# One layer of a hybrid streaming encoder: x enters transposed and unscaled, w_out writes channels on partitions, and the choice of standard and seven-product jobs changes

## Chip, cores and metric

The kernel runs on one core of one Trainium2 chip. The metric is device time in microseconds (us) for one execution; the median of several runs counts. Five things work side by side: TensorE (PE, with its weight loads PEld), VectorE (DVE), ScalarE (ACT), GpSimd (POOL, idle here) and SyncE (SP), which issues all DMAs.

## The reference

A layer for 1024 tokens of 1024 channels, everything in float32:

```
h = rms_norm(x, norm1_w);  proj = h @ w_in            # 1024 -> 7168
q, k, v, g_ret, x_lru, y_lru, gate_ret, gate_lru = split(proj)
y_a = (group_norm(retention(rotary(q), rotary(k), v)) * silu(g_ret)) @ w_ret_o
y_b = (rg_lru(conv(x_lru)) * gelu(y_lru)) @ w_lru_o
mix = sigmoid(gate_ret + b0) * y_a + sigmoid(gate_lru + b1) * y_b
x = x + mix @ w_out
gate, val = split(rms_norm(x, norm2_w) @ ffn_w_up)    # 1024 -> 2 x 3072
x = x + (gelu(conv(gate)) * val) @ ffn_w_down         # 3072 -> 1024
return rms_norm(x, norm_f_w)
```

## The kernel before

**Precision.** Every large product runs in three passes of a 32-bit matmul: each operand is split into a rounded part and the rest (`split`: a ScalarE copy `hi`, L569, and a VectorE subtraction `lo`, L570), and `hi·hi + hi·lo + lo·hi` is accumulated (`PASSES`). A matmul takes a 128x128 stationary block and 512 moving columns.

**Jobs.** The projections are cut into jobs of 256 output channels (28 in w_in, 4 each in ret_o and lru_o, 24 in up; 12 in down, by 3 groups g of 1024 input channels and 4 sets t of token tiles). The weight of a job comes in four blocks A11, A12, A21, A22 (output half, input half), the other operand in B11 to B22 (input half, token half). A *standard* job (`mm_std`, matmuls on L632) makes the four outputs one after the other, 24 matmuls of each. A *fast* job (`mm_fast`, L650) is Winograd's form of Strassen's product: seven block products of 12 matmuls. It takes block sums S1 to S4 of the weight, which VectorE makes in the job (L590 to L599), and T1 to T4 of the operand, which are made once for all jobs that share it; B12 itself occurs in no product. Sums of products are put together in banks X, Y and Z, with copies out by ScalarE (`keep`, L658) and additions on VectorE (`total`, L668). Of one job the products come in the order A11·B11, S1·T1, S2·T2, A12·B21, S3·T3, A22·T4, S4·B22, and `run` puts the first product of the next fast job with the same operand ahead of A22·T4 (`ahead`).

**Stages.** Ahead of the first job `xload` and `norm_half` load x by tokens, take sums of squares, scale the tokens, transpose on TensorE (L749) into channels on partitions and split; `tsets` makes T1 to T4. Then the jobs of w_in in the order of `SEQ`: q, k, v and gate of a head (h), the two branches of the recurrence (x, y), and the merge gates (g); the first STD_L = 2 are standard. Retention and recurrence are side work: generators that `advance` steps on between products, written out to DRAM as og and u. ret_o: 4 standard jobs. lru_o: one standard job, three fast ones. w_out: 384 matmuls (L1174) with mix as the stationary operand, tokens on partitions, first the left 512 output channels, then the right ones; x is added, x1 goes to DRAM, and for each token half `norm_half` normalises and transposes again (L749, tile a). Up: STD_U = 1 standard job, 23 fast. The block sums of w_down are made in the up stage (`down_sums`) and go through DRAM (td). Down: in each of three groups one standard and three fast jobs, adding to x1 in DRAM; the last group ends in the final norm.

**Order.** `record` writes the program down as operations on named tiles. `Prog.plan` goes through them from the end and gives each a latest start; `Prog.run` plays the engines forward with its own durations and takes, for each engine that is free, the ready operation with the earliest latest start. Main TensorE work keeps its order, side work may go between. A tile needs one of 100 buffers of 128x512 (kind u), 6 PSUM banks (g) or 2 for side work (a). What comes out is the fixed instruction order of every engine; on the chip only semaphores decide.

Of the kernel before, what the change touches and what calls it, by code (L numbers as in the profile page):

```python
# [88 lines left out]
class VT:  # L89


    __slots__ = ("kind", "shape", "dt", "acc", "real", "slot", "left", "plan", "name", "whole", "tracked")
# [21 lines left out]
class Ref:  # L114

    __slots__ = ("base", "ops", "shape", "box")

    def __init__(self, base, ops=(), shape=None, box=None):
        self.base, self.ops = base, ops
        self.shape = tuple(base.shape) if shape is None else shape  # L120
        self.box = box

    def __getitem__(self, idx):
        t = idx if isinstance(idx, tuple) else (idx,)
        t = t + (slice(None),) * (len(self.shape) - len(t))
        shape, box = [], []
        for n, i in zip(self.shape, t):
            if isinstance(i, slice):
                a, b, _ = i.indices(n)
                shape.append(b - a)  # L130
                box.append((a, b))
            else:
                box.append((i, i + 1))
        return Ref(self.base, self.ops + (("get", idx),), tuple(shape),
                   tuple(box) if self.box is None and not self.ops else self.box)
# [44 lines left out]
class Op:  # L180

    __slots__ = ("eng", "how", "args", "kw", "occ", "lat", "pred", "succ", "allocs", "uses", "pos", "ls",
                 "start", "ready", "side", "i", "tab", "slack", "dma", "line")
# [17 lines left out]
class Prog:  # L201
# [3 lines left out]
    def __init__(self):  # L205
        self.ops = []
        self.t = 0.0
        self.side = False
        self.slack = None
        self.after = []  # L210

    def add(self, eng, how, args, kw, line):
# [3 lines left out]
        o.side, o.slack = self.side, self.slack  # L216
# [124 lines left out]
    def run(self, caps, trace=None):  # L341
        ops = self.ops
        self.plan()
        STEP = 500.0
# [14 lines left out]
        for v, (s, e) in vts.items():  # L359
            v.plan = s  # L360
            if v.kind == "u":
                occ[bin_(s):bin_(e) + 1] += 1
# [20 lines left out]

        def can(o, t):
            need = [v for v in o.uses if v.slot is None]
            for v in need:
# [3 lines left out]
                if v.kind == "u":  # L390
                    now = t - slip
                    if now < v.plan:
                        if now < v.plan - self.EARLY or len(f) <= self.SPARE:
                            return False
# [5 lines left out]
        def start(o, t):  # L400
# [7 lines left out]
            if o.dma:  # L408
                arrive = max(t + 700, dma_free)
                dma_free = arrive + o.dma / 262144 * 950  # L410
                lat = max(dma_free + 900 - t, 2300.0)
# [5 lines left out]
            for v in o.allocs:  # L417
                _, v.slot = heapq.heappop(free[v.kind])
                if v.kind == "u":
                    now = t - slip  # L420
                    if now < v.plan:
                        occ[bin_(now):bin_(v.plan)] += 1
            for v in o.uses:
                v.left -= 1
                hold[v] = max(hold.get(v, 0.0), done)
                if v.left == 0:
                    heapq.heappush(free[v.kind], (hold[v] + 60, v.slot))
                    heapq.heappush(events, hold[v] + 60)
            for q, l in o.succ:
# [59 lines left out]
        return order  # L489
# [3 lines left out]
    SPARE = 5  # L493
    SWITCH = 1500.0
    LOOK = 12

    def emit(self, engines, make):
        at = {}
        for o in self.order:
# [14 lines left out]
         ("x1", (T, D)), ("td", (3, 4, 4, P, TH)), ("ff", (3, 8, 2, P, 4, P)))  # L514
# [5 lines left out]
STD_L = 2  # L520
STD_U = 1
RATE = 1.0
SEQ = "g g y0 g y1 h0 h1 h2 h3 x0 g g x1 g y2 g x2 g y3 x3"


class Job:

    def __init__(self, src, op, emit, post=None, fast=True, pre=None, fetch=None):
        self.src, self.op, self.emit, self.post = src, op, emit, post
        self.fast, self.pre, self.fetch = fast, pre, fetch  # L530
        self.got = {}

    def take(self, m, h):
        return self.got.pop((m, h)) if (m, h) in self.got else self.fetch(m, h)


def record(prog, fx):
# [4 lines left out]
    og_d, u_d, y_d, sg_d, t1_d, x1_d, td_d, ff_d = (  # L542
        fx[n] for n in ("og_d", "u_d", "y_d", "sg_d", "t1_d", "x1_d", "td_d", "ff_d"))
    x, positions, normf, w_in, w_ro, w_lo, w_out, w_up, w_dn, w_gate, out = (
        fx[n] for n in ("x", "positions", "normf", "w_in", "w_ro", "w_lo", "w_out", "w_up", "w_dn", "w_gate", "out"))
# [61 lines left out]
    def advance(budget):  # L607
        budget *= max(1, len(back))
        while back and budget > 0:
            with within(4000.0, True):  # L610
                c = next(back[0], None)
            if c is None:
# [8 lines left out]
    def mm_std(jb, op):  # L621
        block = blocks(jb)
        for m in range(2):
            for h in range(2):
                ps = bank()
                n = 0
                for k in range(KT):
                    w = block(f"A{m + 1}{k // 4 + 1}")
                    c = slice(128 * (k % 4), 128 * (k % 4) + 128)
                    o = op[f"B{k // 4 + 1}{h + 1}", k % 4]  # L630
                    for a, b in PASSES:
                        PE.matmul(ps, w[a][:, c], o[b], start=n == 0, stop=n == 23)  # L632
                        n += 1
                    if k % 4 == 3:
                        advance(RATE)
                with within(3000.0):
                    jb.emit(m, h, ps, None)

    def mm_fast(jb, op):
# [3 lines left out]
        def prod(ps, an, bn, first):  # L643
            w = block(an)
            n = 0
            for j in range(4):
# [14 lines left out]
        def more(u, m, c):  # L661
            if jb.pre is not None and (m, c) in jb.pre:
                with within(3000.0):
                    V.tensor_add(u, u, jb.take(m, c))
# [17 lines left out]
        u3 = keep(X)  # L682
        more(u3, 1, 1)
        total(u3, Z, 1, 1)
        yield
# [3 lines left out]
        more(u2, 0, 1)  # L689
        prod(Z, "S4", "B22", False)  # L690
        total(u2, Z, 0, 1)

    def run(jobs):
        ahead = None
        for jb, nx in zip(jobs, jobs[1:] + [None]):
            if jb.fast:
                g = ahead
                if g is None:
                    g = mm_fast(jb, jb.op)
                    next(g)  # L700
                next(g)
                ahead = None
                if nx is not None and nx.fast and nx.op is jb.op:
                    ahead = mm_fast(nx, nx.op)
                    next(ahead)
                next(g, None)
            else:
                mm_std(jb, jb.op)
            if jb.post is not None:
                g = jb.post()  # L710
                if g is not None:
                    back.append(g)
# [12 lines left out]
    def rms_scale(tiles, n, o=0):  # L725
        for t in range(n):
            for c in range(2):
                j = bank("a")
                if c == 0:
                    S.activation(j, tiles[t, c], AF.Square, accum_out=nst[:, c, o + t:o + t + 1])  # L730
                else:
                    V.scalar_tensor_tensor(j, tiles[t, c], 1.0, tiles[t, c], ALU.mult, ALU.mult,
                                           accum_out=nst[:, c, o + t:o + t + 1])
        a, b, v, r, w = (nst[:, i, o:o + n] for i in range(5))
        V.tensor_add(v, a, b)
        V.tensor_scalar(v, v, 1.0 / D, EPS, ALU.mult, ALU.add)
        rstd_of(r, v, w)
        return r

    def norm_half(tiles, wname, op, half, keep, wide=False):  # L740
        r = rms_scale(tiles, 4)
        for c in range(2):
            for t in range(4):
                V.tensor_scalar(tiles[t, c], tiles[t, c], r[:, t:t + 1], None, ALU.mult)
        for k in range(KT):
            ps = bank("g" if wide else "a")
            for t in range(4):
                c0 = 128 * (k % 4)
                PE.transpose(ps[:, 128 * t:128 * t + 128], tiles[t, k // 4][:, c0:c0 + 128], ident)  # L749
            w = pc(wname, k)  # L750
            hi, lo, f = get("hh", F32R), get("hl", F32R), get("hf")
            if k % 2 == 0:
                S.activation(hi, ps, AF.Copy, scale=w)
                V.scalar_tensor_tensor(lo, ps, w, hi.bitcast(F32), ALU.mult, ALU.subtract)
                S.activation(f, ps, AF.Copy, scale=w)
            else:
                S.activation(f, ps, AF.Copy, scale=w)
                V.tensor_copy(hi, f)
                V.tensor_sub(lo, f, hi.bitcast(F32))
            op[f"B{k // 4 + 1}{half + 1}", k % 4] = (hi, lo)  # L760
            keep[f"B{k // 4 + 1}{half + 1}", k % 4] = f
# [14 lines left out]
    def xload(half):  # L776
        tl = {}
        for t in range(4):
            for c in range(2):
                b = get("xt")  # L780
                r0 = 512 * half + 128 * t
                SY.dma_start(b, x[r0:r0 + 128, 512 * c:512 * c + 512])
                tl[t, c] = b
        return tl

    h1, keep = {}, {}
# [107 lines left out]
    def lru_block(n, xl):  # L894
# [7 lines left out]
        for h in range(2):  # L902
# [45 lines left out]
            for m in range(2):  # L948
# [15 lines left out]
                yield 1.7  # L964

# [76 lines left out]
    def ret_out(hd, gg):  # L1042
        for h in range(2):
            for m in range(2):
# [7 lines left out]
                yield 0.8  # L1052

    def emit_gate(which, n):
        def emit(m, h, src, unit):
            t = get("sg") if unit is None else unit
            S.activation(t, src, AF.Sigmoid, bias=pc("merge_gate_b", 8 * which + 2 * n + m))
# [3 lines left out]
    def operand(op, fetch, sums=True):  # L1061
# [3 lines left out]
        if sums:  # L1065
            tsets(op, fetch)
# [26 lines left out]
    def emit_ret_o(n):  # L1093
        def emit(m, h, ps, unit):
            t = ojobs[n].take(m, h)
# [4 lines left out]
    def emit_lru_o(n):  # L1100
        def emit(m, h, ps, unit):
            g, t = ojobs[4 + n].take(m, h)
# [7 lines left out]
    def add(i, emit, post=None):  # L1110
        jobs.append(Job(pair_src(w_in, i), h1, emit, post, fast=len(jobs) >= STD_L))

    gates = [(w, n) for n in range(4) for w in range(2)]
    for what in SEQ.split():
        if what == "g":
            w, n = gates.pop(0)
            add(20 + 4 * w + n, emit_gate(w, n))
# [13 lines left out]
    def start_tables():  # L1131
        lru_constants()
        return rotary_tables()
# [3 lines left out]
    ojobs = [Job(pair_src(w_ro, n), og, emit_ret_o(n), fast=False, fetch=from_sg(0, n)) for n in range(4)]  # L1137
# [264 lines left out]
```

## Time and profile before

| | us |
|---|---|
| median of 3 runs (1661.72 to 1663.68) | 1662.11 |
| the profiled execution | 1663.31 |
| its span, first to last instruction | 1661.5 |
| TensorE busy in the span | 1623.5 |
| VectorE busy | 1244.3 |
| ScalarE busy | 881.1 |
| first matmul of a job | 31.59 |
| end of the last matmul | 1653.4 |

How to read the views: a group is "line engine operation out<-in shapes xcount | busy us, mean ns of one | idle time before them and what ended it". In the chain and the timeline the first number is the start in us from the span's start, the second the length. In a table of windows each engine has its busy time with a count. Matmuls overlap, so the time that one adds to a full stream is the distance of two starts, not its duration.

### The profile page before, as it was taken

Reading aid. Unit: us, or ns where it says so; the run is one execution under the profiler, and the core shown is the slowest. Engines: PE = TensorE matmul, PEld = TensorE weight load, DVE = VectorE, ACT = ScalarE, POOL = GpSimd, SP = SyncE. Lnnn points to the kernel's source line nnn. Section 1 sums busy time; section 2 is a strip of 40 time slices with the busy share of each in tenths; the row PEclk is TensorE's granted clock in tenths of the full one; section 3 lists DMA queues with packets and bytes.
Section 4 is the critical chain, followed back from the end, with each engine's and each line's share of the span. In section 5 each row is a group of like instructions: output and inputs, shape, how many; then the busy total and the mean of one; then the engine's idle time right before and its main releaser. Section 6 shows DMA issues by size and latency. Waiting matters only on the chain.

```text
span 1661.5 us, 21070 instructions
## 1 busy us (share of the span) xinstructions
PE 1623.5 (98%) x7284; PEld 1339.1 (81%) x7284; DVE 1244.3 (75%) x2295; ACT 881.1 (53%) x1468; POOL 0.2 (0%) x4
## 2 busy tenths in 40 slices
PE   4999999999999999999999999999999999999997
PEld 4888888888888888888888788888888888888886
DVE  7986475766768887876882897777777777877786
ACT  6473434344578878863440464444444546544464
POOL 0000000000000000000000000000000000000000
PEclk9999999999999999999999999999999999999999
DMA  5343131322233336369454424344444448686862
GB/s 194 102 127 95 45 93 48 89 78 63 81 129 112 115 106 247 116 219 328 145 181 154 145 74 142 123 143 129 150 146 134 146 129 264 244 280 237 292 220 77
DMA packets 153804, 246.95 MB, mean 149 GB/s; under 512 B 15328, under 2 KB 40032, under 8 KB 153696
## 3 DMA queue, kind: packets, MB, share of 16 engines
q1 hardware_dynamic: 153696, 245.60, 45.2%
q8 instruction: 57, 0.93, 0.2%
q14 instruction: 51, 0.42, 0.1%
HBM read 173.19 MB, written 67.11 MB: 145 GB/s over the span
## 4 chain that ended last, share of the span: by engine, by line
PE 92%; ACT 4%; DVE 2%; DMA 1%; issue 1%; SPq 0%; DVEq 0%; ACTq 0%
PE g L650 68%; PE g L632 13%; PE g L1174 5%; PE a L928 2%; PE a L1018 1%; PE a L1025 1%; PE a L1017 1%; PE a L749 0%; PE a L1011 0%; PE a L1048 0%; PE a L1000 0%; DMA xt<-x 0%; ACT L947 0%; PE g L749 0%; DVE wl L570 0%
## 5 line engine op out<-in xcount | busy, mean ns | idle before, releaser
L650 PE MATMUL g<-bh,wh 128*128 128x512 f32 x1120 | 441.7, 394 | 3.5 <-ACT pk L658 3.4
L650 PE MATMUL g<-bh,wl 128*128 128x512 f32 x1120 | 440.2, 393 | 1.0 <-DVE wl L570 0.9
L650 PE MATMUL g<-bl,wh 128*128 128x512 f32 x1120 | 439.8, 393 | 0.2 <-DVE bl L570 0.2
L650 PEld LDWEIGHTS g<-bh,wh 128*128 128x128 f32 x1120 | 210.3, 188 | 48.4 <-ACT pk L658 5.9
L650 PEld LDWEIGHTS g<-bh,wl 128*128 128x128 f32 x1120 | 210.3, 188 | 45.5 <-DVE wl L570 3.0
L650 PEld LDWEIGHTS g<-bl,wh 128*128 128x128 f32 x1120 | 210.4, 188 | 42.7 <-DVE bl L570 0.7
L650 PE MATMUL g<-hh,wh 128*128 128x512 f32 x588 | 231.0, 393 | 0.0
L650 PE MATMUL g<-hh,wl 128*128 128x512 f32 x588 | 230.8, 393 | 0.0
L650 PE MATMUL g<-hl,wh 128*128 128x512 f32 x588 | 230.6, 392 | 0.0
L658 ACT COPY pk<-g 128x512 f32<-128x512 f32 x183 | 107.4, 587 | 218.5 <-PE g L650 212.8
L668 DVE TENSOR_TENSOR pk<-g,pk 128x512 f32<-128x512 f32 x183 | 126.2, 690 | 127.8 <-PE g L650 113.0
L569 ACT CAST wh<-wr 128x512 fp32r<-128x512 f32 x288 | 172.5, 621 | 67.1 <-DMA wr<-w_up 31.9
L570 DVE TENSOR_TENSOR wl<-wr,wh 128x512 fp32r<-128x512 f32 x288 | 194.6, 684 | 4.2 <-ACT wh L569 4.2
L569 ACT CAST wh<-ws 128x512 fp32r<-128x512 f32 x183 | 113.0, 620 | 87.1 <-DVE ws L590 34.8
L570 DVE TENSOR_TENSOR wl<-ws,wh 128x512 fp32r<-128x512 f32 x183 | 124.5, 685 | 8.7 <-ACT wh L569 8.3
L650 PEld LDWEIGHTS g<-hh,wl 128*128 128x128 f32 x588 | 110.5, 188 | 22.8 <-DVE wl L570 0.3
L650 PEld LDWEIGHTS g<-hh,wh 128*128 128x128 f32 x588 | 110.4, 188 | 22.7
L650 PEld LDWEIGHTS g<-hl,wh 128*128 128x128 f32 x588 | 110.5, 188 | 22.3
L632 PE MATMUL g<-bh,wh 128*128 128x512 f32 x256 | 99.7, 389 | 0.4 <-ACT wh L569 0.4
L632 PE MATMUL g<-bh,wl 128*128 128x512 f32 x256 | 99.7, 389 | 0.1
L632 PE MATMUL g<-bl,wh 128*128 128x512 f32 x256 | 99.6, 389 | 0.0
L1196 ACT ACTIVATE gc<-pk,par 128x512 f32<-128x512 f32 x46 | 37.6, 817 | 72.3 <-DVE pk L668 72.3
(239 smaller groups left out, 2275.8 us busy)
## 6 DMA issues: line engine op xcount, KB each, us to landing
wr<-w_in SPq DMA_DIRECT2D x112, 256.0 KB, 2.9
wr<-w_up SPq DMA_DIRECT2D x96, 256.0 KB, 3.2
ds<-w_dn SPq DMA_DIRECT2D x48, 256.0 KB, 4.1
td_d<-ds SPq DMA_DIRECT2D x48, 256.0 KB, 2.3
ff_d<-gc SPq DMA_DIRECT2D x48, 256.0 KB, 2.5
dw<-w_dn SPq DMA_DIRECT2D x48, 256.0 KB, 4.6
wr<-ff_d SPq DMA_DIRECT2D x48, 256.0 KB, 5.3
x<-x_d SPq DMA_DIRECT2D x48, 256.0 KB, 5.1
```

What stands on the lines that cost most here:

```text
L569: S.copy(hi, src)
L570: V.tensor_sub(lo, src, hi.bitcast(F32))
L632: PE.matmul(ps, w[a][:, c], o[b], start=n == 0, stop=n == 23)
L650: PE.matmul(ps, w[a][:, c], o[b], start=first and n == 0, stop=n == 11, skip_group_check=True)
L658: S.copy(u, ps)
L668: V.tensor_add(u, ps, u)
L928: PE.matmul(ps, wg[g][a][:, cs], xs[k][b], start=q == 0, stop=q == 5)
L1017: PE.matmul(p2[:, 0:256], qk[0, h][:, bs], rst[cur], start=True, stop=False)
L1018: PE.matmul(p2[:, 0:256], s, v, start=first, stop=True)
L1025: PE.matmul(p3[:, 0:256], kd[h][:, bs], v, start=True, stop=True)
L1174: PE.matmul(ps, o[a][:, 128 * t:128 * t + 128], wo[k][b], start=n == 0, stop=n == 23)
L1196: S.activation(c, src, AF.Identity, bias=pc("ffn_conv_b", i), scale=pc("ffn_conv_w", 48 + i))
```

## The change

Four parts, and changes of the planner beside them.

1. **x transposed.** A second copy of x, `xt` with channels on partitions, is laid out as an input. `start_transposed` loads it, multiplies by norm1_w and splits it without 1/rms; this unscaled operand `h1u` feeds the first STD_L = 4 jobs, which are now all merge gates and multiply their outputs by 1/rms of the tokens (`rrow`). Meanwhile x is loaded by tokens for the sums of squares (ScalarE alone), `rows_of` spreads 1/rms over the partitions by products with ones, and the scaled operand h1 with its T1 to T4 is made for the fast jobs.
2. **w_out with channels on partitions.** It becomes four standard jobs over weight pairs; the outputs are added to xt, transposed by tokens only for x1 and for the sums of squares (`turn`), and scaled in place by `rrow`.
3. **Which jobs are fast.** Down: all 12 (before 9); lru_o: all 4 (before 3); ret_o: 3 of 4 (before none); w_in: 24 of 28 (before 26); up: 22 of 24 (before 23). T1 to T4 of og and u are made in the generators of the last two heads and blocks by `sums_of`, go through DRAM (`to`) and are loaded by `sums_from`.
4. **Order of products.** Standard jobs that share an operand run as a group, token half by token half; a fast job copies Z early, ends in S4·B22, A22·T4, and no product of the next job comes ahead.

```diff
-STD_L = 2
-STD_U = 1
-RATE = 1.0
-SEQ = "g g y0 g y1 h0 h1 h2 h3 x0 g g x1 g y2 g x2 g y3 x3"
+STD_L = 4
+STD_U = 2
+STD_W = 4
+STD_RO = 1
+STD_LO = 0
+RATE = 2.5
+SLACK = 45000.0
+SEQ = "g g g g y0 y1 h0 x0 y2 h1 x1 g y3 h2 x2 g h3 x3 g g"
...
+    def mm_std(group):
+        made = [blocks(jb) for jb in group]
+        for h in range(2):
+            for jb, block in zip(group, made):
+                ps = [bank(), bank()]
                 for k in range(KT):
...
+                    for m in range(2):
+                        w = block(f"A{m + 1}{k // 4 + 1}")
+                        for i, (a, b) in enumerate(PASSES):
+                            PE.matmul(ps[m], w[a][:, c], o[b], start=k == 0 and i == 0, stop=k == 7 and i == 2)
...
         prod(X, "A11", "B11", True)
         s1 = keep(X)
-        yield
+        more(s1, 0, 0)
         prod(Z, "S1", "T1", True)
+        z = keep(Z)
+        more(z, 1, 1)
         prod(X, "S2", "T2", False)
         u2 = keep(X)
-        more(s1, 0, 0)
+        more(u2, 0, 1)
         prod(Y, "A12", "B21", True)
         total(s1, Y, 0, 0)
         prod(X, "S3", "T3", False)
-        u3 = keep(X)
-        more(u3, 1, 1)
-        total(u3, Z, 1, 1)
-        yield
+        total(z, X, 1, 1)
+        prod(Z, "S4", "B22", False)
+        total(u2, Z, 0, 1)
         prod(X, "A22", "T4", False)
...
+    def rows_of(r, side):
+        one = sm()
+        V.memset(one, 1.0)
+        for h in range(2):
+            with within(1000.0, side):
+                row = bank()
+                for t in range(4):
+                    dg = sm()
+                    V.tensor_scalar(dg, ident, r[:, 4 * h + t:4 * h + t + 1], None, ALU.mult)
+                    PE.matmul(row[:, 128 * t:128 * t + 128], one, dg, start=True, stop=True)
+                rrow[h] = get("row")
+                S.copy(rrow[h], row)
+
+    def start_transposed():
+        raw = {}
+        for h in range(2):
+            for k in range(KT):
+                t = raw[k, h] = get("xc")
+                SY.dma_start(t, xt[k, :, TH * h:TH * h + TH])
+                hi, lo = get("hh", F32R), get("hl", F32R)
+                S.activation(hi, t, AF.Copy, scale=pc("norm1_w", k))
+                V.scalar_tensor_tensor(lo, t, pc("norm1_w", k), hi.bitcast(F32), ALU.mult, ALU.subtract)
+                h1u[f"B{k // 4 + 1}{h + 1}", k % 4] = (hi, lo)
+        prog.floor = 23000.0
+        for t in range(8):
             for c in range(2):
...
+                b = get("xs")
+                SY.dma_start(b, x[128 * t:128 * t + 128, TH * c:TH * c + TH])
+                S.activation(b, b, AF.Square, accum_out=nst[:, c, t:t + 1])
...
+        rows_of(r, True)
+        for j in range(4):
+            for n in ("B11", "B12", "B22", "B21"):
...
+                V.scalar_tensor_tensor(t, t, pc("norm1_w", k), rrow[h], ALU.mult, ALU.mult)
...
+        if hd >= 2:
+            for j in (2 * hd - 4, 2 * hd - 3):
+                yield from sums_of(from_dram(og_d), to_d[0], j)
...
+    def turn(t, ch0, nch, part, sums):
+        ps = bank("a")
+        for i in range(nch):
+            PE.transpose(ps[:, 128 * i:128 * i + 128], x1t[ch0 + i, t // 4][:, 128 * (t % 4):128 * (t % 4) + 128],
+                         ident)
+        o = get("x1s")
+        S.copy(o[:, :128 * nch], ps[:, :128 * nch])
+        SY.dma_start(x1_d[128 * t:128 * t + 128, 128 * ch0:128 * ch0 + 128 * nch], o[:, :128 * nch])
+        S.activation(ps[:, :128 * nch], ps[:, :128 * nch], AF.Square, accum_out=sums[:, part, t:t + 1])
```

In the planner an operation can carry a `floor`, a time before which its latest start isn't set (23 us for the loads and sums of x and all that follows up to h1, 60 us for side work); loads may be issued up to 20 us ahead of their planned place (`FETCH`), the price of a table switch on ScalarE rises from 1.5 to 6 us (`SWITCH`), two buffers instead of five are kept spare, and the buffers of ended tiles are counted free again.

More of the change, by code (lines that the diff above doesn't have):

```diff
@@ L339, in plan, with run, forward @@
                     push(q)
-    def run(self, caps, trace=None):
+    def run(self, caps):
+        best = None
+        for _ in range(int(self.ROUNDS)):
+            try:
+                self.forward(caps)
+            except RuntimeError as e:
+                if best is None and _ == self.ROUNDS - 1:
+                    raise
+                print(str(e)[:60])
+                break
+            if best is None or self.span < best[0]:
+                best = self.span, self.order, [(v, v.slot) for o in self.order for v in o.allocs], [
+                    (o, o.start, o.allocs) for o in self.order]
+            t = 0.0
+            for o in self.ops:
+                if o.eng == "PE" and not o.side:
+                    t = max(t, o.start)
+                    o.pos = t
+                    t += o.occ
+                else:
+                    o.pos = t
+        self.span, self.order, slots, starts = best
+        for v, i in slots:
+            v.slot = i
+        for o, t, a in starts:
+            o.start, o.allocs = t, a
+        return self.order
+    def forward(self, caps):
         ops = self.ops
         self.plan()
+        for o in ops:
+            o.ls = max(o.ls, o.floor)
+            o.start = None
+            for v in o.uses:
+                v.slot, v.left = None, 0
         STEP = 500.0
@@ L428, in start @@
                     heapq.heappush(events, hold[v] + 60)
+                    if v.kind == "u":
+                        now = logical(hold[v] + 60)
+                        if now < v.end:
+                            occ[bin_(now) + 1:bin_(v.end) + 1] -= 1
             for q, l in o.succ:
@@ L688, in mm_fast, with after @@
             jb.emit(1, 0, X, None)
-        more(u2, 0, 1)
-        prod(Z, "S4", "B22", False)
-        total(u2, Z, 0, 1)
+    def after(jb):
+        g = jb.post() if jb.post is not None else None
+        if g is not None:
+            back.append(g)
     def run(jobs):
-        ahead = None
-        for jb, nx in zip(jobs, jobs[1:] + [None]):
+        jobs = deque(jobs)
+        while jobs:
+            jb = jobs.popleft()
             if jb.fast:
[L697 to L712, printed above, removed]
+                mm_fast(jb, jb.op)
+                after(jb)
+                continue
+            group = [jb]
+            while jobs and not jobs[0].fast and jobs[0].op is jb.op:
+                group.append(jobs.popleft())
+            mm_std(group)
     def pair_src(w, i):
@@ L740, in norm_half, with sums_of @@
[L740 to L761, printed above, removed]
+    def sums_of(fetch, dst, j):
+        b = {(kh, c): fetch(f"B{kh + 1}{c + 1}", j) for kh in range(2) for c in range(2)}
+        yield 1.0
+        t = get("ds")
+        V.tensor_sub(t, b[0, 1], b[0, 0])
+        SY.dma_start(dst[0, j], t)
+        yield 1.0
+        V.tensor_sub(b[0, 1], b[1, 1], b[0, 1])
+        SY.dma_start(dst[2, j], b[0, 1])
+        yield 1.0
+        V.tensor_sub(b[1, 1], b[1, 1], t)
+        SY.dma_start(dst[1, j], b[1, 1])
+        yield 1.0
+        V.tensor_sub(b[1, 0], b[1, 0], b[1, 1])
+        SY.dma_start(dst[3, j], b[1, 0])
+        yield 1.0
@@ L763, in tsets, with sums_from @@
+    def sums_from(op, src):
+        for i in range(4):
+            for j in range(4):
+                t = get("td")
+                SY.dma_start(t, src[i, j])
+                op[f"T{i + 1}", j] = split(t, "b")
     def tsets(op, fetch):
@@ L1191, in post_ff @@
+    channel_major()
+    gvs = [{} for _ in range(FF // P)]
     def post_ff(i):
+        gv = gvs[i]
         g, kh, kk = i // 8, (i % 8) // 4, i % 4
@@ L1249, in fn @@
                 post_ff(i)
-            return down_sums(i // 8, i % 8 // 2) if i % 2 == 0 else None
+            return sums_of(down_of(i // 8), td_d[i // 8], i % 8 // 2) if i % 2 == 0 else None
         return fn
-    run([Job(pair_src(w_up, i), h2, emit_to(gv, "gv"), up_post(i), fast=i >= STD_U) for i in range(NF)])
+    run([Job(pair_src(w_up, i), h2, emit_to(gvs[i], "gv"), up_post(i), fast=i >= STD_U) for i in range(NF)])
     drain()
```

314 lines of the change are left out of this document (157 added, 157 removed).

## Prediction

> **What bounds the kernel now.** I read the page first, its shares of busy time and its chain that ended last.
>
> ```profile
> PE 1623.5 (98%) x7284; PEld 1339.1 (81%) x7284; DVE 1244.3 (75%) x2295; ACT 881.1 (53%) x1468; POOL 0.2 (0%) x4
> ...
> PE 92%; ACT 4%; DVE 2%; DMA 1%; issue 1%; SPq 0%; DVEq 0%; ACTq 0%
> ```
>
> TensorE carries 92% of the chain. How full it is says the chain in order of time (start, length, what), not the 98%, because matmuls overlap.
>
> ```profile
> 31.67 43.74 PE g L632 x192
> ...
> 851.11 70.50 PE g L1174 x311
> ...
> 961.89 12.99 PE g L632 x56
> 974.88 432.49 PE g L650 x1908
> ...
> 1653.37 0.69 DVE pk L668
> ...
> 1657.37 0.72 ACT pk L1301
> ```
>
> From 974.88 on, 1908 matmuls run in 432.49 us without a gap: 0.2267 us for each, and the first two jobs (192 in 43.74) have 0.228. This is the price of a matmul while nothing else holds it up. The run has three other parts: 31.6 us ahead of the first matmul, the waits between stages, and 8.1 us from the last matmul's end (1653.4) to the end of the span, 1661.5. The waits of TensorE come next (total, times, longest).
>
> ```profile
> PE g L749 <- DVE nst L735: 18.5, 1, 18.5
> PE g L650 <- ACT pk L658: 3.4, 5, 0.7
> ```
>
> Only the start is a long one. The five of L650 are the accumulation in X that must be copied before product A22·T4 adds to it. A third loss stands in no row of its own: from 851.11 to 974.88 (w_out, second norm, first up job) are 123.8 us, for 384 + 96 = 480 matmuls (108.8 us) and 64 transposes.
>
> ```profile
> 18.50:21.70 3.20, 3.20 (x15) 3.20 (x16) 2.80 (x12) 2.46 (x5) 0.00 (x0) 1.00 1.05 304
> 21.70:23.50 1.80, 1.80 (x18) 1.80 (x17) 1.80 (x6) 1.71 (x4) 0.00 (x0) 1.00 1.04 384
> 851.10:974.90 123.80, 120.99 (x546) 98.47 (x545) 78.04 (x153) 44.56 (x82) 0.00 (x0) 0.97 0.42 135
> ```
>
> (Windows: length; busy of PE, weight load, DVE, ACT, POOL with counts; clock, DMA share, GB/s.) A transpose takes up to 0.11 us once TensorE is warm (18 in 1.80), the 64 some 7.0, so 8.0 us of that stretch are waits.
>
> **The change, part by part.** *Matmuls.* A standard job is 4 outputs of 24 = 96, a job in seven products 7 × 12 = 84. The groups of the trace give the count before.
>
> ```profile
> L650 PE MATMUL g<-bh,wh 128*128 128x512 f32 x1120 | 441.7, 394 | 3.5 <-ACT pk L658 3.4
> ...
> L650 PE MATMUL g<-hh,wh 128*128 128x512 f32 x588 | 231.0, 393 | 0.0
> ...
> L632 PE MATMUL g<-bh,wh 128*128 128x512 f32 x256 | 99.7, 389 | 0.4 <-ACT wh L569 0.4
> ```
>
> (1120 + 588) × 3 = 5124 = 61 jobs of 84; the 256 are one of three passes of 8 standard jobs, 3 + 4 + 1 in down, ret_o and lru_o. The change: the projection has 4 standard jobs for 2 (+24 matmuls), ret_o 1 for 4 (-36), lru_o 0 for 1 (-12), up 2 for 1 (+12), down 0 for 3 (-36); w_out keeps 384. Net -48 × 0.2267 = **-10.9 us**.
>
> *Start.* Normalising, transposing and splitting x goes from ahead of the first matmul to beside the four standard jobs, which take x transposed unscaled. What is left ahead: load params, one tile of xt and two weight blocks, cast, split.
>
> ```profile
> 3.50 0.70 DVE L732 SCALAR_TENSOR_TENSOR a<-xt 128x512 f32<-128x512 f32 x1 [2.08 <-DMA xt<-x]
> ...
> 16.15 0.60 ACT L730 ACTIVATE a<-xt 128x512 f32<-128x512 f32 x1 [0.69 <-DMA xt<-x]
> ...
> 18.81 0.60 ACT L569 CAST wh<-wr 128x512 fp32r<-128x512 f32 x1
> 19.45 0.69 DVE L570 TENSOR_TENSOR wl<-wr,wh 128x512 fp32r<-128x512 f32 x1
> ```
>
> The first of 16 tiles is in at 3.50, the last at 16.15: 0.84 us each. The third lands at 5.2; cast and split (0.60 + 0.69) make it 6.5 for the second output, 4.4 + 0.6 = 5.0 for the first matmul. After that TensorE takes 6 matmuls for each tile of xt (1.36 us), more than the 0.84 of a landing, so it isn't starved: tile 12, which the last step of the first job needs, is in at 12.7. I count 5.8 us, and 1.6 for a slow start of TensorE: its first 15 transposes took 3.20 us, 0.213 each, the next 18 half of that each (the clock column says 1.00 for both). So the start is worth 31.6 - 7.4 = **-24.2 us**, with ends of 5.0 and 12 (the loads of x, 16 tiles, going ahead of the weights would add 5) for the moment from which matmuls stream. The Trainium skill, "TensorE: Matmul & The Clock Gate", Part 4, says that transposes do not count as activity that raises the clock. By that rule the first matmuls of before were cold already, and the 1.6 us would not be new; but here the transposes alone brought the full rate, after 3.2 us, and the matmuls have it from 31.67 on, so the measurement decides.
>
> *Row of 1/rms.* Sixteen fp32 products of 128 columns, each two instructions.
>
> ```profile
> 181.39 0.38 PE L1011 MATMUL a<-pk,qk 128*128 128x128 f32 x2
> ```
>
> 0.22 to 0.38 us each, so 3.5 to 6.1: **+4 us**. The 64 transposes of the first norm lay ahead of the first matmul and are within the 24.2; those of the second norm stay 64.
>
> *Second norm.* Sums of squares are taken from transposes during the second token half of w_out, and the half h = 0 of two grouped up jobs (2 × 48 × 0.2267 = 21.8 us) covers the scaling of h = 1. The chain after the last w_out product is some ten steps of 0.2 to 0.7 us and a table load, near 10 us, below 21.8. Of the 8.0 I leave 2: **-6 us**. Ends -8 and 0. The new order of products puts S4·B22 or A12·B21 between every read of X and the next write: **-3.4 us**, ends -3.4 and 0.
>
> *What is late next.* The standard jobs that go were where VectorE caught up.
>
> ```profile
> 1485.14 2.49 DVE L570 TENSOR_TENSOR bl<-dw,bh 128x512 fp32r<-128x512 f32 x4
> ```
> ```profile
> 1394.00:1413.80 19.80, 19.12 (x84) 15.52 (x84) 17.65 (x30) 12.30 (x22) 0.00 (x0) 1.00 1.03 370
> ...
> 1474.00:1493.60 19.60, 18.93 (x84) 15.36 (x83) 17.01 (x28) 8.50 (x15) 0.00 (x0) 1.00 0.98 345
> 1493.60:1515.40 21.80, 21.80 (x98) 18.06 (x97) 15.41 (x25) 11.97 (x22) 0.00 (x0) 1.00 0.91 336
> ```
>
> (Four splits in 2.49: 0.60 us each.) Where one operand follows another (ret_o to lru_o, up to down, and twice within down) two fast jobs now meet, 38.1 us. VectorE has 2 × (7 splits + 4 block sums + 3 totals + 4 other adds) = 36 operations and 28 splits of the new operand that are used: 64 × 0.60 = 38.4 us, 40.8 with the four of B12 that nothing reads. DMA has 32 + 2 × 12 = 56 tiles of 0.262 MB, 39.7 us at 370 GB/s. Before, 16 of the splits lay in the last job and the other 16 had the standard job. Splitting ahead is shown to work, so I take 1.5 us a place, the size by which both sums run over; ends 0 and 8.6 (nothing ahead: 28 × 0.60 less the 8.2 us that 18 operations leave free in one job). Four places: **+6 us**, ends 0 and 34. The Trainium skill, "DMA: Bandwidth & Descriptors", Specifications, gives a fabric ceiling of 435 GB/s and an HBM limit near 358 for a core. By the first the 56 tiles would need 33.7 us (an estimate) and DMA would hold up nothing; by the second 41.0, 2.9 over. The window's 370 lies by the second, and the sum goes by it.
>
> *Entry to the fast jobs.* The scaled operand needs the row of 1/rms, which needs x: about 40 tiles of 0.84 plus 3.5, so 40 us. Then VectorE has 16 scalings, 28 splits, 16 differences, 16 gate products, 8 weight splits and the first fast job's 11: 95 × 0.60 = 57, done by 97, where that job begins at 7.4 + 4 × 21.8 = 94.6 and needs its last operands 16 us later. **+2 us**, ends 0 and 19 (the 32 differences and their splits all behind the fourth job).
>
> ```profile
> 31.60:75.40 43.80, 43.80 (x194) 36.28 (x194) 43.80 (x85) 23.81 (x40) 0.00 (x0) 1.00 0.25 79
> 75.40:683.00 607.60, 606.09 (x2779) 500.80 (x2777) 438.34 (x864) 365.82 (x571) 0.00 (x0) 1.00 0.32 102
> 683.00:851.00 168.00, 166.98 (x733) 136.89 (x732) 134.66 (x221) 91.02 (x142) 0.00 (x0) 1.00 0.62 213
> ```
>
> *Costed at nothing.* The 32 differences of the sums for og and u (19 us), with about 25 us of the recurrence that now lies ahead of ret_o, go into the projection: 438 + 44 of 570 us (two fast jobs fewer than in the window), 85% of VectorE. In 31.6 to 75.4 it was busy without a break and TensorE lost nothing. ret_o and lru_o come to 230 operations, 138 of 155 us. The new ScalarE work (12 more jobs' casts and copies, the gate copies) has 40% of its time free there. The +48 tiles of traffic for og and +32 for u have two thirds of the DMA time in the projection. If that cover is gone, rival 2 tells the price. What waits anew on SP's queue are 32 writes of sums on VectorE's differences and 24 writes of x1 parts on ScalarE's copies; loads of weights and operands stand behind them.
>
> ```profile
> td_d<-ds SPq DMA_DIRECT2D x48, 256.0 KB, 2.3
> ```
>
> The same kind of write, 48 times in the up stage, delayed no matmul there (none of its waits is in TensorE's list). The end stays 8.1.
>
> **Sum**, against the profiled run's 1663.3 (span 1661.5 and 1.8 around it): -24.2 - 10.9 + 4 - 6 - 3.4 + 6 + 2 = -32.5, so 1630.8. The median shown is 1662.1, 1.2 lower, so, rounded, **1630 us**.
>
> **The rivals.** *1: VectorE and DMA become the bound where operands change.* For it: the window at 1394 has DMA full, and 64 operations need all of 38.1 us. Against it: only 28 operations were done in the 19.6 us at 1474, with room for four more. At 5 us a place (20 in all, 14 more than counted): 1644. *2: the projection fills VectorE.* For it: 85% on average, with the recurrence in clumps. Against it: 72% (438 of 608) cost 1.5 us of TensorE. If a third of the added 44 us finds no idle VectorE, some 15: 1645. *3: the early start does not hold:* the loads come in an order by which matmuls stream only from 20 us. For it: one SP queue issues all of them. Against it: 0.84 us a tile is faster than 1.36. 12.6 us lost: 1643. *4, slower: no buffers are free.* One hundred tiles hold 56 of the old operand, at the entry also 32 unscaled, 32 of weights and 16 of raw xt; if new splits can only begin when the old ones are released, the four places cost 34 and the entry 19, 45 over what is counted: 1675. It decides from waits of some 40 us in all on. Against it: 16 splits (32 tiles) were ready ahead of the standard jobs. *5:* all waits vanish: the 2 + 6 + 2 left above: 1620.
>
> **How the numbers follow.** Chances: the forecast with waits from 0 to 20 us (1620 to 1640, rival 5 within it) 0.62, rival 1 0.14, rival 2 0.08, rival 3 0.07, rival 4 0.09. 0.2% (3.3 us) is about what a measurement of this kernel can tell from no change; below 1658.8 lie the forecast and rivals 1 to 3, so faster 0.91; rival 4 has 0.03 for same (some 30 us of its waits) and 0.06 for slower. The range 1618 to 1649 leaves out rival 4 and the late parts of 1 to 3.
>
> **What would show it.** First F32R matmul near 5 us and an even stream from 8. 6516 matmuls of 512 columns in the three groups, at 0.227. No wait of L650's kind on the copy of X. Between w_out and up, TensorE idle below 2 us. TensorE's waits at the four places on the splits of bl or their loads: 1.5 us each, 5 by rival 1, 8 by rival 4. DVE busy near 80% of a shorter span. I am wrong if TensorE idles over 20 us in all after the first matmul, or if the first matmul comes after 12.

## The result, and the profile after

The changed kernel takes 1625.14 us (median; 1624.96 to 1628.01), the one before beside it 1662.89: a ratio of 0.9777, 95% interval 0.976 to 0.9794. The forecast was 1630 with a range of 1618 to 1649. The profiled execution is the longest of the four, 1628.01 with a span of 1626.2; the kernel run a second time on another occasion gave 1624.83 and a profile with a span of 1622.7. One of the four executions of the experiment with ret_o in standard jobs took 4167 us and is left out of its time below.

The page of the changed kernel, busy time by engine and the groups of matmuls:

```profile
PE 1603.8 (99%) x7204; PEld 1325.8 (82%) x7204; DVE 1294.9 (80%) x2360; ACT 925.9 (57%) x1592; POOL 0.2 (0%) x4
...
L704 PE MATMUL g<-bh,wl 128*128 128x512 f32 x1556 | 612.9, 394 | 0.4 <-DVE wl L620 0.4
...
L704 PE MATMUL g<-hh,wl 128*128 128x512 f32 x264 | 102.8, 389 | 0.0
...
L684 PE MATMUL g<-hh,wh 128*128 128x512 f32 x192 | 76.7, 399 | 9.6 <-ACT wh L619 9.6
...
L684 PE MATMUL g<-bl,wh 128*128 128x512 f32 x160 | 63.2, 395 | 0.0
```

Fast jobs have (1556 + 264) × 3 = 5460 = 65 × 84 matmuls, standard ones (192 + 160) × 3 = 1056 = 11 × 96: together 6516, 48 fewer, as counted. VectorE has 50 us more work in a span 35 us shorter. The chain of the changed kernel in order of time:

```profile
2.10 5.08 DMA wr<-w_in
7.20 0.62 ACT wh L619
7.87 24.30 PE g L684 x93
...
674.05 21.76 PE g L684 x96
...
830.05 64.60 PE g L684 x285
...
970.81 647.37 PE g L704 x2856
1618.20 0.69 DVE x L1370
```

The last long row is the clearest: 22 fast jobs of up and all 12 of down, 34 × 84 = 2856 matmuls, in 647.37 us, 0.2267 each. In 40% of the kernel TensorE waits for nothing, the three changes of operand in it included. From the starts of the stages and the counts follows what each stage has beyond its matmuls at 0.2267 us and its small products at their measured distances (0.108 to 0.215 us):

| | before | after |
|---|---|---|
| ahead of the first matmul of a job | 31.6 | 7.9 |
| standard jobs of w_in, without the rows of 1/rms | 0.3 | 5.8 |
| fast jobs of w_in with retention and recurrence | 5.6 | 8.3 |
| ret_o and lru_o | 2.8 | 0.7 |
| w_out, second norm, standard jobs of up | 7.7 | 1.2 |
| the rest of up, and down | 3.8 | 0 |
| after the last matmul | 8.1 | 8.0 |

The list of TensorE's waits (total, times, longest):

```profile
PE g L684 <- ACT wh L619: 9.6, 2, 7.9
PE a L1001 <- ACT lg L1004: 1.1, 1, 1.1
PE a L1101 <- DVE state L1103: 0.9, 1, 0.9
PE g L704 <- ACT pk L712: 0.9, 1, 0.9
```

The first is the start (7.9) and one wait of 1.7 near 32 us. Windows of the changed kernel show both, and the two places in down that the prediction feared (columns as before):

```profile
7.87:14.01 6.14, 6.14 (x14) 4.74 (x15) 5.82 (x9) 5.79 (x9) 0.00 (x0) 1.00 1.05 393
14.01:30.00 15.99, 15.99 (x72) 13.22 (x71) 4.19 (x7) 11.97 (x33) 0.00 (x0) 1.00 1.05 387
30.00:35.00 5.00, 3.27 (x15) 2.32 (x13) 0.79 (x3) 3.78 (x12) 0.00 (x0) 1.00 1.04 372
...
1370.80:1389.90 19.10, 19.10 (x86) 15.84 (x85) 18.51 (x33) 15.04 (x27) 0.00 (x0) 1.00 0.99 337
1389.90:1408.90 19.00, 19.00 (x86) 15.74 (x85) 18.46 (x32) 11.23 (x21) 0.00 (x0) 1.00 0.99 355
```

In the first row 14 matmuls take 6.14 us, 0.44 each; in the second 72 take 16.0, 0.222. In the last two, around the change from up to down, VectorE is busy 97% and DMA 99%, and TensorE 100%.

### The profile page after: what moved, and what is told of

It is laid out like the page before. It is cut to its first block, busy times and chain, and to the rows that moved or that the text cites. A ratio compares the mean times of both kernels' runs of the same rounds, so it can differ in the third digit from the quotient of the medians.

```text
span 1626.2 us, 21515 instructions
## 1 busy us (share of the span) xinstructions
PE 1603.8 (99%) x7204; PEld 1325.8 (82%) x7204; DVE 1294.9 (80%) x2360; ACT 925.9 (57%) x1592; POOL 0.2 (0%) x4
## 4 chain that ended last, share of the span: by engine, by line
PE 91%; ACT 3%; DMA 3%; DVE 2%; issue 1%; SPq 0%; ACTq 0%; DVEq 0%
PE g L704 71%; PE g L684 14%; PE a L1001 2%; PE a L1094 1%; PE a L1093 1%; PE a L1101 1%; DMA bf<-u_d 1%; DMA wr<-w_lo 1%; DMA sg_d<-pk 0%; ACT L1004 0%; PE a L1124 0%; PE a L1087 0%; ACT L1014 0%; ACT lg L1004 0%; PE a L1254 0%
## 5 line engine op out<-in xcount | busy, mean ns | idle before, releaser
L704 PE MATMUL g<-bh,wl 128*128 128x512 f32 x1556 | 612.9, 394 | 0.4 <-DVE wl L620 0.4
L704 PE MATMUL g<-bh,wh 128*128 128x512 f32 x1556 | 612.2, 393 | 0.9 <-ACT pk L712 0.9
L704 PE MATMUL g<-bl,wh 128*128 128x512 f32 x1556 | 612.0, 393 | 0.0
L704 PEld LDWEIGHTS g<-bh,wh 128*128 128x128 f32 x1556 | 292.5, 188 | 60.4 <-ACT pk L712 1.5
L704 PEld LDWEIGHTS g<-bh,wl 128*128 128x128 f32 x1556 | 292.4, 188 | 60.5 <-DVE wl L620 1.2
L704 PEld LDWEIGHTS g<-bl,wh 128*128 128x128 f32 x1556 | 292.5, 188 | 59.5
L704 PE MATMUL g<-hh,wl 128*128 128x512 f32 x264 | 102.8, 389 | 0.0
L704 PE MATMUL g<-hl,wh 128*128 128x512 f32 x264 | 102.8, 389 | 0.0
L704 PE MATMUL g<-hh,wh 128*128 128x512 f32 x264 | 102.8, 389 | 0.0
L684 PE MATMUL g<-hh,wh 128*128 128x512 f32 x192 | 76.7, 399 | 9.6 <-ACT wh L619 9.6
L1320 DVE SCALAR_TENSOR_TENSOR gc<-pk,par,gc 128x511 f32<-128x511 f32 x88 | 65.6, 746 | 23.0 <-ACT gc L1317 22.6
L684 PE MATMUL g<-hl,wh 128*128 128x512 f32 x192 | 76.4, 398 | 0.0
L684 PE MATMUL g<-hh,wl 128*128 128x512 f32 x192 | 76.3, 397 | 0.0
L684 PE MATMUL g<-bl,wh 128*128 128x512 f32 x160 | 63.2, 395 | 0.0
L684 PE MATMUL g<-bh,wl 128*128 128x512 f32 x160 | 63.1, 394 | 0.0
```

The lines of the kernel that those rows point to most:

```text
L684: PE.matmul(ps[m], w[a][:, c], o[b], start=k == 0 and i == 0, stop=k == 7 and i == 2)
L704: PE.matmul(ps, w[a][:, c], o[b], start=first and n == 0, stop=n == 11, skip_group_check=True)
L1320: V.scalar_tensor_tensor(c[:, s:], src[:, :TH - s], w, c[:, s:], ALU.mult, ALU.add)
```

## The experiments

All are the changed kernel with one edit. The kernel before was measured beside each of the three groups of runs (1663.2, 1663.0, 1664.6 us), so ratios to it are given: 0.977 (0.9756 to 0.9785) is the unaltered changed kernel, 1624.83 us. A difference with a sign is that of the two times; in the third group, whose kernel before is 1.4 us slower, that by the ratio is given too.

**The same kernel once more** (no edit).

> The changed kernel once more, unaltered, to see what one execution differs by. Theory 1 (the stream of TensorE is the bound from the entry to the end, and the profiled 1628.0 against 1625.1 of the other executions is the slow-clock phase at the start, 15 matmuls at 0.43 us in that trace): an execution near 1625 has some 2 us less between the first matmul and the start of the first fast job (94.9 us in the trace), and the rest of the stages within 0.5 us. Rival (waits in the projection differ from run to run): the 94.9 us stay and the 571 us of the projection are 2 to 3 shorter.

1624.83 us. In this profile the first matmul starts at 6.86, 1.0 us earlier than in the other, and ret_o at 671.26 for 674.05; the span is 3.5 shorter.

```profile
6.86 23.95 PE g L684 x93
...
671.26 21.76 PE g L684 x96
827.25 64.60 PE g L684 x285
```

From first matmul to first fast job it is 94.4 for 94.7 us, though 10 matmuls and not 14 were slow. So neither theory: 1.0 came ahead of the first matmul, 0.4 in the standard jobs, 1.4 in the projection, 0.7 behind. Profiles of one program differ by 3 us, in small waits all over.

**Down with a standard job in each group.**

```diff
-                 emit_down(g, t), pre=((0, 0), (0, 1), (1, 1)), fetch=from_x1(t))
+                 emit_down(g, t), fast=t > 0, pre=((0, 0), (0, 1), (1, 1)), fetch=from_x1(t))
```

> The first job of each down group is standard again, 36 matmuls more. Theory 1 (TensorE's stream is the bound there, VectorE and DMA have room at the operand changes): 36 x 0.2267 = +8.2 us, about 1633. Theory 2 (VectorE and DMA are at their limit where operands change, as the sums 64 x 0.60 = 38.4 and 39.7 us against 38.1 said): the standard jobs give back the 1.5 to 5 us a place that the change lost, so +8.2 less 4.5 to 15, that is 1618 to 1629.

1633.91 us, ratio 0.9823 (0.9809 to 0.9838): +8.8 us against +8.2 by the matmuls. Theory 1; the all-fast groups lost nothing at their borders.

**ret_o standard, lru_o with one standard job.**

```diff
-STD_RO = 1
-STD_LO = 0
+STD_RO = 4
+STD_LO = 1
```

> ret_o has four standard jobs again and lru_o one, as before: 48 matmuls more. The sums of og go through DRAM still and are loaded, but not used. Theory 1: 48 x 0.2267 = +10.9 us, about 1636. Theory 2: DMA moved 350 GB/s in the 79 us of ret_o and was busy 0.98 of it; with 10 us more for the same bytes waits go away, so less than +8.

1639.4 us, ratio 0.9858 (0.9838 to 0.9877): +14.6, more than either theory. The matmuls are 10.9 of it. The rest is at the entry to ret_o, by the chain of this run:

```profile
656.50 5.27 DMA bf<-og_d
661.83 4.83 DMA wr<-w_ro
666.71 4.17 DVE bl L620 x7
...
682.31 5.43 DMA wr<-w_ro
687.77 0.62 ACT wh L619
```

Here operand loads and weight loads are links of the chain, and TensorE loses 4.6 us from 655 to 843, where ret_o and lru_o of the changed kernel lose 0.9. Four jobs with one operand go as a group by token half, so all their weights are wanted in the first half, on top of the 32 tiles of the operand. What the removal of these standard jobs is worth is thus no less than their matmuls.

**The old start**, with norm, transposes and split ahead of the four standard jobs; `h1u` is `h1`, the gates are not scaled.

```diff
-    start_transposed()
+    for half in range(2):
+        norm_half(xload(half), "norm1_w", h1, half, keep, True)
+    tsets(h1, lambda n, j: keep[n, j])
```

> The start of before (x by tokens, norm, transposes, split) ahead of the four standard jobs, which take the scaled operand; the rest as after. Theory 1 (the part is worth the difference of the two starts by the traces: 31.6 less 7.9, of which the slow clock, one wait of 1.9 us and the rows give back 6 to 8): +16 to +18 us, about 1642. As the prediction had it: +20 (24.2 less the 4 of the rows, of which only the first 1.8 go away, less 2), about 1647. Rival (the entry to the fast jobs bounds, so that an early start is lost there): below +10.

1642.04 us, ratio 0.9874 (0.986 to 0.9889): +17.2 us, the largest part of the gain, as theory 1 had it by the traces, and 3 below the prediction's net. In this run the first matmul comes at 31.7 and the first fast job 87.7 us later, where 384 matmuls need 87.1:

```profile
31.69:119.34 87.65, 87.46 (x384) 72.10 (x385) 61.35 (x129) 37.64 (x64) 0.00 (x0) 1.00 0.22 73
```

The early start needs 94.4. So of the 24.8 us that the first matmul gains, 6.7 go back in the standard jobs: 1.8 for the products of the row, 2 to 3 for slow first matmuls, 1.9 for one wait, and the rest in small ones.

**The old w_out**, tokens on partitions, with `norm_half` behind it and the weights laid out as before; two standard up jobs stay.

```diff
-    channel_major()
+    mix = {(k, h): split(mixf[k, h], "mx") for k in range(KT) for h in range(2)}
...
+    for c in range(2):
...
+            if c == 1:
+                with within(None, True):
+                    norm_half(tl, "norm2_w", h2, half, keep2)
```

> w_out and the second norm as before (tokens on partitions, norm_half behind it), with the two grouped up jobs of after; the 384 matmuls stay, the 16 products of the row of 1/rms go (-1.8 us). Theory 1: the waits of that stretch come back, 8.0 less the 1.2 that the changed kernel's trace has, less 1.8 for the rows: +5 us, about 1630. As the prediction had it: 6 - 2 = +4. Rival (two grouped standard jobs in up cover the second half's norm in the old form as well, so that it is STD_U and not the layout that gains): +0 to +1.5.

1624.37 us, ratio 0.9767 (0.9753 to 0.9782): no difference. The stretch from w_out to the first fast job, in this run and, in the second fence, in the changed kernel (windows):

```profile
828.20:967.40 139.20, 138.68 (x641) 114.04 (x641) 86.08 (x167) 55.45 (x100) 0.00 (x0) 1.00 0.37 118
```

```profile
830.00:970.80 140.80, 140.17 (x658) 116.03 (x657) 75.28 (x140) 63.29 (x148) 0.00 (x0) 1.00 0.26 84
```

Without the 8 products of the row (16 instructions) it is 1.6 us shorter, and TensorE is busy but for some half a microsecond in both. The new layout of w_out is worth nothing in time; it takes 11 us of work from VectorE and gives ScalarE 8.

**One standard up job** shows what took the waits out instead.

```diff
-STD_U = 2
+STD_U = 1
```

> Only the first up job is standard, so the second token half of the norm is covered by 48 matmuls (10.9 us) and not by 96 (21.8); 12 matmuls fewer. Theory (the grouped pair of standard jobs is what took the waits out of the second norm, since the old w_out with the pair cost nothing): the fast jobs need T1 to T4 21.8 us earlier, 16 differences and 16 splits of VectorE besides 32 for the scaled halves; the waits of before come back in part, -2.7 and +5 to +8, so +2 to +5, near 1628. Rival (grouping by token half is enough with one job as well): -2.7, 1622.

1631.06 us, ratio 0.9801 (0.9786 to 0.9815): +6.2, or +5.2 by the ratio, with 12 matmuls fewer. So 8 to 9 us of losses come back, at or somewhat above the upper end of what the theory expected. The list of TensorE's waits has the place, and a window behind the longest wait shows what the list leaves out:

```profile
PE g L684 <- DVE hl L620: 3.7, 1, 3.7
...
PE g L704 <- DVE bl L620: 1.0, 2, 0.6
```

```profile
937.30:944.13 6.83, 5.50 (x13) 4.34 (x14) 6.83 (x13) 4.59 (x9) 0.00 (x0) 0.50 0.14 38
```

The split of the second token half (hl) is late for a job that has only 10.9 us of the first half to cover it, and the T sums (bl) are late for the first fast job. Two grouped jobs, 21.8 us a half, cover both, in either layout. Not all of the loss is waiting: in the window the granted clock is 0.50, and its 13 matmuls start 0.43 us apart for most, not 0.227, which is some 2.7 us more. The kernel before has the same at this place:

```profile
950.20:957.03 6.83, 6.27 (x22) 4.67 (x23) 5.64 (x12) 5.32 (x9) 0.00 (x0) 0.50 0.30 95
```

The changed kernel and the old w_out with the pair have a clock of 1.00 over the whole stretch.

**Three standard jobs at the start.**

```diff
-STD_L = 4
+STD_L = 3
```

> Three jobs on the unscaled operand for four: 12 matmuls fewer, 2.7 us. Theory 1 with the entry bound by VectorE (it is busy 95% from 45 to 102 us in the changed kernel, and the last splits for the first fast job end at 107.4, when they are needed): the entry comes 21.8 us earlier than the scaled operand, so of the 19.05 + 2.7 gained most turns into waits; +10 to +17 us, 1635 to 1642. Rival (the planner had simply spread the work to the time there was, and it fits in less): -2.7, about 1622.

1626.67 us, ratio 0.9785 (0.9769 to 0.9802): within the noise of the changed kernel, +1.8. Both theories miss. Windows of this run:

```profile
45.00:76.60 31.60, 31.60 (x143) 26.21 (x142) 30.85 (x51) 25.78 (x47) 0.00 (x0) 1.00 0.33 117
76.60:102.00 25.40, 22.45 (x88) 15.63 (x87) 25.26 (x44) 12.11 (x21) 0.00 (x0) 1.00 0.26 88
```

The first fast job starts at 76.6 instead of 102.6. Now VectorE is at its limit (25.26 of 25.40) and TensorE waits some 5 us in the second window, which eats the 2.7 us of the matmuls and little more. The same 57 us in the changed kernel:

```profile
45.00:102.00 57.00, 57.00 (x253) 47.22 (x252) 54.18 (x95) 38.83 (x67) 0.00 (x0) 1.00 0.26 92
```

VectorE has 95 operations there in both runs. So of those that the changed kernel does ahead of its first fast job, 95% busy, part could wait: busy time alone did not show a limit.

**Four more VectorE operations in each down job**; their output is not used.

```diff
         u2 = keep(X)
+        if jb.pre is not None:
+            du = get("du")
+            with within(1200.0):
+                for _ in range(4):
+                    V.tensor_sub(du, u2, u2)
```

> Each of the 12 down jobs gets four more VectorE subtractions that nothing uses, 4 x 0.60 = 2.4 us in 19.05, 28.8 us in all; the output stays. Theory 1 (room at the operand changes): within 2 us of 1625. Theory 2 (64 of 0.60 us fill the 38.1 us of two jobs): 72 operations are 43.2 us, 5 late at each of the three places and at the end, +10 to +15.

1635.35 us, ratio 0.9835 (0.982 to 0.9849): +10.5 for 28.8 us of work. Theory 2 has the size, but not the places: 5.3 us are lost at the border of up and down, 2.4 and 2.8 at the two within down, nothing at the end. Waits, and a window at the first border:

```profile
PE g L704 <- DVE bl L620: 4.8, 10, 1.1
PE g L704 <- DVE wl L620: 1.1, 2, 0.7
```

```profile
1390.00:1410.00 20.00, 16.66 (x68) 11.74 (x66) 20.00 (x35) 12.17 (x24) 0.00 (x0) 1.00 1.05 380
```

TensorE starts 68 matmuls where 88 fit; VectorE is busy 20.00 of 20.00. So the all-fast groups have room for the work that they have, and less than 2.4 us a job more: the bound that the prediction saw is there, just not reached.

**The last two products changed round.**

```diff
-        prod(Z, "S4", "B22", False)
-        total(u2, Z, 0, 1)
         prod(X, "A22", "T4", False)
         with within(1500.0):
             jb.emit(1, 0, X, None)
+        prod(Z, "S4", "B22", False)
+        total(u2, Z, 0, 1)
```

> The last two products of a fast job change places: A22.T4, which adds to X, comes straight behind the addition that reads X. Theory 1 (a read of X with nothing in between costs TensorE what it cost before at the five places, 0.84 us from the last product to the next by the trace): 65 jobs x 0.84 = +55 us, about 1680. Rival (VectorE reads X early enough, or side work fills the gap): below +20.

1702.6 us, ratio 1.0239 (1.0223 to 1.0254): +77.8 us, 1.2 us a job, slower than the kernel before. A line of the waits and one pause in the timeline of this run:

```profile
PE g L704 <- DVE pk L722: 55.4, 52, 2.4
```

```profile
1666.52 0.39 PE L704 MATMUL g<-bh,wl 128*128 128x512 f32 x1
1667.69 0.50 PE L704 MATMUL g<-bh,wh 128*128 128x512 f32 x1 [0.78 <-DVE pk L722]
```

1.17 us from start to start where 0.23 is the rule. It is the shortest in up and down: each of their 34 fast jobs has such a pause, up to 2.77 us, and this part of the run loses 60 us in all. Four of these pauses, of 2.15 to 2.77 us, are followed by a fall of the granted clock, here behind one that ends at 1042.50:

```profile
1043.95:1047.37 3.42, 3.42 (x9) 2.67 (x9) 0.00 (x0) 0.53 (x2) 0.00 (x0) 0.50 0.00 0
```

Eight matmuls start 0.43 us apart there (the ninth in the count began before), some 1.6 us lost each time. The kernel before hid this read of X behind a product of the next job; the new order hides it inside the job. It is a condition of the whole result, though beside the before kernel it gains only the 2.5 us of the few places without a next job.

**Warming TensorE.** Twenty fp32 products of ones ahead of the first matmul.

```diff
+    hot, hots = sm(), bank()
+    V.memset(hot, 1.0)
+    prog.t = 0.0
+    for _ in range(20):
+        PE.matmul(hots[:, 0:128], hot, hot, start=True, stop=True)
+    prog.t = prog.BEGIN
     start_transposed()
```

> Twenty small fp32 products of a tile of ones go ahead of the first matmul, from about 1 us on; nothing uses their output. Theory 1 (7 to 14 first matmuls at 0.43 us are the slow clock of an idle TensorE, 0.2 us lost on each): none of the matmuls at 0.43, -1.4 to -2.8 us, about 1622.5. Rival (the slow matmuls wait for weights or operands at the start): still 0.43 for the first ones, no change.

1626.53 us, ratio 0.9773 (0.9757 to 0.979): +1.7, or +0.5 by the ratio, no gain. The timeline of this run:

```profile
1.04 6.48 PE L1233 MATMUL g<-sc 128*128 128x128 f32 x40 [1.04 <-DVE sc L1230]
...
8.22 0.40 PE L684 MATMUL g<-hh,wh 128*128 128x512 f32 x1
8.45 0.40 PE L684 MATMUL g<-hl,wh 128*128 128x512 f32 x1
...
9.87 0.53 PE L684 MATMUL g<-hl,wh 128*128 128x512 f32 x1 [0.28 <-DVE hl L834]
```

Locally theory 1 holds: the matmuls of 0.43 us are gone, two starts are now 0.23 apart. But TensorE then waits for the splits of x, and the first fast job starts at 100.1, 1.1 us earlier than in the second profile of the changed kernel, which the later stages lose again.

**The sums of squares later, consts behind the first weights.**

```diff
+    prog.floor = 15000.0
     SY.dma_start(cst, fx["consts"])
+    prog.floor = -1e9
...
-        prog.floor = 23000.0
+        prog.floor = 32000.0
```

> The latest starts of the sums of squares get a floor of 32 us for 23, and the load of consts one of 15 us, so that ScalarE has the weight casts of the third standard job ahead of most squares and the first weight block is loaded ahead of consts. Theory 1: the wait of 1.9 us near 31 us goes, and the first matmul comes 0.85 us (0.33 MB at 388 GB/s) earlier: -2.7, about 1622; 1/rms comes some 4 us later, and if VectorE has no room for that at the entry (95% busy from 45 to 102 us), waits of up to 4 us there give it back. Rival: all given back, 1625.

1622.24 us, ratio 0.9746 (0.9731 to 0.9761): -2.6, or -4.0 by the ratio, but its interval overlaps that of the changed kernel, so the time alone does not show the gain. The chain of this run begins so:

```profile
1.64 3.40 DMA wr<-w_in
5.73 36.26 PE g L684 x147
```

The first matmul starts at 5.73, and 147 matmuls follow without the pause near 31 us, which was ScalarE's order: squares and a copy stood ahead of a weight cast whose tile had been loaded. The first fast job starts at 97.5, for 102.6 and 101.2, and the entry did not take that back. Which of the two edits gave what wasn't run apart: of the 3.7 us to the earlier of the two starts, 1.1 lie ahead of the first matmul and 2.6 in the standard jobs, where the pause was.

**Both** (the edits of the last two).

> Both of the last two together. If they are independent, -4 to -5.5, about 1620; if the entry to the fast jobs takes back what the start gains, not below 1622.5.

1621.52 us, ratio 0.9742 (0.9727 to 0.9756), the fastest here: 3.3 us below the changed kernel, 4.7 by the ratio. The intervals just touch; the first fast job at 96.7 agrees with a gain. By the medians the larger part comes from the later sums; that the warming adds to it is not shown, 0.7 us being within the noise.

No run undoes the new order of jobs or the changes of the planner by themselves; what they are worth stays open.

## Why the prediction was right

*What bounds.* Right: TensorE's stream, at 0.2267 us a matmul in both kernels, and the sum of counts and losses gives the span in both.

*Matmuls, -10.9.* Right, count and price: 6516, and 36 put back cost 8.8 us for 8.2.

*Start, -24.2, and entry, +2.* The mechanism was right, the size too large by some 3 us. Net of the first rows and the entry the prediction has 20.4, the old start put back costs 17.2. The term that was mis-sized is the streaming from 5.8 us with 1.6 for a slow clock. The first matmul came at 6.5 to 7.9: its weight block was issued at 2.10 and landed at 7.2, behind consts, where I had counted three tiles of 0.84 us. The slow matmuls were 7 to 14 of 0.43 us, 1.4 to 2.8 us lost, for the 1.6 that was counted. And the wait of 1.7 behind the squares on ScalarE had no term. The Trainium skill, "TensorE: Matmul & The Clock Gate", Part 1, puts the slow phase at about 3.4 us of a free-running window, with 6, 11 or 14 slow matmuls in runs of one kernel; the count agrees, but 14 of them took 6.1 us here, well over that window.

*Rows, +4.* By the counted distances 1.8 at each place, 3.6.

*Second norm, -6.* Right in size (7.7 to 1.2) and half wrong in cause. The prediction named two things, sums from transposes during w_out and the cover of two grouped up jobs; the runs give all of it to the pair: without the new layout nothing changes, without the pair 8 to 9 us come back. And the 8.0 us that the prediction took for waits were not all waits: its own window of that stretch has the clock at 0.97, and from 950.20 to 957.03 it was 0.50.

*Copies of X, -3.4.* 2.5 by the waits that are left; the order is worth 78 us to a kernel that no longer draws the next job's product ahead.

*Operand changes, +6.* This term failed: 0 in up and down, 0.7 in ret_o and lru_o. The 1.5 us a place were the amount by which both sums ran over 38.1 us, and neither did. At the change from up to down the splits begin with the last job, as the sum had it, and go on into the first job of down (1371.1 to 1404.5); 63 operations of VectorE start in the two jobs, for the 64 of the sum, and in the windows it is busy 37.0 us of 38.1. DMA moved 13.2 MB in them, not the 14.7 of 56 tiles, the others lying outside. So it fits, without room to speak of. The four extra operations show that it was near: less than 2.4 us a job.

*The other rivals.* 2 (projection): 8.3 us lost for 5.6, a small part of its 15. 3: matmuls streamed from 14 us at the latest, not from 20, but for the one pause near 32. 4: no sign of it.

The errors were +6 or so at the start and -8 at the borders and the entry. That they offset each other is luck: the total came out 5 us from the measured one, closer than its terms.

## What to carry to other kernels

Where one engine's stream is the bound, count its instructions, take the price from a long row without gaps, and look for the loss stage by stage; busy shares of the other engines near 100% aren't a limit until an added operation shows it. When a gain has two possible causes in one edit, undo them one by one: here the layout got the credit for what a scheduling constant did. An engine's order can hold up the critical one for work that isn't urgent; here sixteen squares stood ahead of a weight cast, and with them moved back by 9 us a pause of 1.9 us was gone.

## What the runs showed of the hardware

At the start the clock column says 1.00 while matmuls of 512 columns start 0.43 us apart, and later 0.227; this first slow phase can be seen only in the distances. Small fp32 products end it as matmuls do. In the stream a slow phase can come back behind a pause, and there the column has it at 0.50: for 6.83 us behind a pause of 4.04 us from start to start (one standard up job), for 3.4 us behind pauses of 2.15 to 2.77 (products swapped). The length of the pause alone does not decide it: one of 2.63 us, at 1438.6 in the same run, brought none. DMA held 387 to 393 GB/s for 22 us in the changed kernel's start, all loads; the Trainium skill, "DMA: Bandwidth & Descriptors", section "Where 436 GB/s comes from", has HBM bind a load at some 358, a core's share, while its measurement for a core alone reaches 425; in this kernel, on one core, the first does not bind.
